# Gated linear attention: a head's output norm placed behind the next head's first score factors, one multiplication per step

## The chip, the cores and the metric

The kernel runs on one core of a Trainium2 chip. The metric is the device time of one execution in microseconds (us), taken as the median of several runs. Before the change it is 2079.0 us (three runs, 2078.53 to 2080.28).

The engines have these names in the profile: PE is TensorE's matmul, PEld its weight load, DVE is VectorE, ACT is ScalarE, POOL is GpSimd, SP is the queue that issues most DMAs.

## What is computed

One layer of a trunk: a gated linear attention mixer (512 tokens, model width 2048, 4 heads with 256 key and 512 value columns) and a SwiGLU feed-forward. The part that matters here is the mixer, cut to its core:

```python
def gla_mixer(h, w_in, w_a2, b_a, g_norm, w_out):
    q, k, v, r, a_lr = split(h @ w_in)
    log_a = log_sigmoid(a_lr @ w_a2 + b_a) / GLA_TAU
    ...
    scores = einsum('bhtd,bhsd,bhtsd->bhts', qb, kb, decay)   # decay = exp(b_t - b_s), s <= t
    o_intra = einsum('bhts,bhsv->bhtv', scores, vb)
    ...
    o = rms_norm(o, g_norm).reshape(B, S, GLA_DV) * silu(r)   # per head, over its 512 value columns
    return o @ w_out
```

The output norm of a head is `rms_norm(o)`: a sum of squares over the head's 512 value columns, the inverse root of their mean, and a multiplication of every output element with it.

## The kernel before

All of a head is done for the 512 tokens at once, with scores for every pair of tokens; no state is carried. Each head goes through these steps:

- `project_qk(h)`: 8 chunks of two weight tiles each, of 24 matmuls per chunk, into four banks; then VectorE writes q and k (L303, L305).
- `log_gate(h)` and `decays(h, b)`: the running sums of the log gates (tile PX, extended from level to level by `advance`: GpSimd L339, VectorE L340, by turns) and the exponentials made from them (kt for the keys, qt for the queries: L351 to L361).
- `scores(h, ...)`: in four levels, for blocks of 2, 8, 32 and 128 tokens. In each, `factors` multiplies the exponentials with k on GpSimd (kt, L406) and with q on VectorE (qt, L407 to L409); `products` are the matmuls of kt and qt on TensorE (L436, for the last level L495), and `take` copies them under a mask into the score tile Sd (VectorE, L454 and L458). The diagonal is a product by itself (GpSimd L417 and L418, TensorE L423, VectorE L425). "First factors" and "first products" below are those of blocks of 2, the second those of blocks of 8.
- `project_v(h)`: again 8 chunks, for the values.
- `attend(h, ...)`: scores times values into oT[h], with the sum of squares in the tile so. At its end it appends `finish`, the head's output norm: a matmul of so with ones (`rms_rows`, L215), then `rsqrt` (VectorE L161, ScalarE L162 and L163, VectorE L164 to L167) into the tile Rh, then four multiplications of oT[h] with Rh on GpSimd (L540).

Every weight chunk comes by DMA as a raw tile and is split into two parts: hi (ScalarE, L121) and lo (VectorE, L122). Three such pairs are in flight.

What sets the order: the projections' matmuls are written straight through by `group`, and after every second column of a chunk (12 matmuls) it calls `tick()`. A tick takes one step from the generator in front of the list `queue` and one step from the one in front of the list `side`. `scores` and `attend` stand in `queue`; `finish`, the diagonal's `take` and the next head's `log_gate` stand in `side`, one behind the other. So head h's scores and head h-1's norm are written between the matmuls of head h's projections. Each engine works through its own instructions in the order in which they were written.

Pools that matter: products, norm sums and diagonals take turns in three PSUM banks (`mis_ps`); the tiles kt, qt, PX, so and Rh exist once each.

Of the kernel before, what the change touches and what calls it, by code (L numbers as in the profile page):

```python
# [18 lines left out]
H = 4  # L19
# [22 lines left out]
def trunk_kernel(ctx: ExitStack, tc: tile.TileContext, x, xT, cst, masks, wa2r, w_in, w_out, w_gu, w_down, out):  # L42
# [22 lines left out]
    def mis_bank():  # L65
        return mis_ps.tile([P, G], F32, tag="mis", name="mis")

    def temp(n=S):
        return tmp.tile([P, S], F32, tag="t", name="t", bufs=4)[:, 0:n]
# [61 lines left out]
    def prod3(out, a, b, start, stop):  # L131
        (ah, al), (bh, bl) = a, b
        nc.tensor.matmul(out, ah, bh, start=start, stop=False)  # L133
        nc.tensor.matmul(out, ah, bl, start=False, stop=False)  # L134
        nc.tensor.matmul(out, al, bh, start=False, stop=stop)  # L135
# [22 lines left out]
    def rsqrt(src_ps, n, y, temps=None):  # L158

        a, t = temps or (temp(y.shape[1]), temp(y.shape[1]))  # L160
        nc.vector.tensor_scalar(a, src_ps, 1.0 / n, EPS, ALU.mult, ALU.add)  # L161
        nc.scalar.activation(t, a, AF.Ln)  # L162
        nc.scalar.activation(y, t, AF.Exp, scale=-0.5)  # L163
        nc.vector.tensor_mul(t, y, y)  # L164
        nc.vector.tensor_mul(t, t, a)
        nc.vector.tensor_scalar(t, t, -0.5, 1.5, ALU.mult, ALU.add)
        nc.vector.tensor_mul(y, y, t)  # L167
# [5 lines left out]
    def add_square(dst, src, first):  # L173
        if first:
            nc.gpsimd.tensor_mul(dst, src, src)
        else:
            sq = temp()
            nc.scalar.activation(sq, src, AF.Square)
            nc.gpsimd.tensor_add(dst, dst, sq)
# [33 lines left out]
    def rms_rows(src, n, dst):  # L213
        b = mis_bank()
        nc.tensor.matmul(b, ones, src, start=True, stop=True)  # L215
        yield
        rsqrt(b, n, dst)
# [72 lines left out]
        yield  # L290


    scored = []

    def project_qk(h):

# [98 lines left out]
    def scores(h, q, k, sc):  # L395
# [18 lines left out]
        def diagonal():  # L414
            e = temp()
            ev = e.rearrange("p (c t) -> p c t", c=2)
            nc.gpsimd.tensor_mul(ev, q[:, :, 0:S:2], k[:, :, 0:S:2])  # L417
            nc.gpsimd.tensor_add(e[:, 0:256], e[:, 0:256], e[:, 256:512])  # L418
            return e
# [43 lines left out]
        f = factors(2, *first_decays[h])  # L463
        yield
        e = diagonal()
        m0 = 0
        for b in LEVELS:
            advance(h, b)
# [42 lines left out]
    def attend(h, v, sc):  # L511
        (vh, vl, v3), (Sd, Sh, Sl) = v, sc
        ot = ob.tile([P, 4, G], F32, tag=f"ob{h}", name=f"oT{h}")
        oT.append(ot)
        so = gl.tile([P, S], F32, tag="so", name="so")

        def take(vt, b):
            nc.scalar.activation(oT[h][:, vt, :], b, AF.Copy)
            add_square(so, oT[h][:, vt, :], vt == 0)

        b = None
        for vt in range(4):
            prev, b = b, mis_bank()
            vs = slice(vt * P, (vt + 1) * P)
            for j, o in enumerate((0, 512, 896)):
                r = slice(o, o + (4 - j) * P)
                prod3(b[:, j * P :], (vh[:, j, vs], vl[:, j, vs]), (Sh[:, r], Sl[:, r]), j == 0, False)
            nc.tensor.matmul(b[:, 384:512], v3[:, vs], Sd[:, 384:512], start=False, stop=True)
            if prev is not None:
                take(vt - 1, prev)  # L530
            yield
            yield
        take(3, b)

        def finish():
            Rh = gl.tile([P, S], F32, tag="Rh", name="Rh")
            yield
            yield from rms_rows(so, HV, Rh)
            for vt in range(4):
                nc.gpsimd.tensor_mul(oT[h][:, vt, :], oT[h][:, vt, :], Rh)  # L540

        side.append(finish())

    queue.append(start())
    gates, oT, first_decays = [], [], []
    for h in range(H):
        q, k = project_qk(h)
        if h == 0:
            queue.append(log_gate(h))
        Sc = (  # L550
            gl.tile([P, S], F32, tag="Sd", name="Sd"),
            gl.tile([P, 1152], F32R, tag="Sh", name="Sh"),
            gl.tile([P, 1152], F32R, tag="Sl", name="Sl"),
        )
        queue.append(scores(h, q, k, Sc))
        v = project_v(h)
        queue.append(attend(h, v, Sc))
# [630 lines left out]
```

## Time and profile before

| | |
|---|---|
| median of three runs | 2079.0 us |
| the profiled execution, its own time | 2078.67 us |
| its span, first to last instruction | 2076.9 us |
| PE busy | 2063.1 us, 99% |
| DVE busy | 1597.9 us, 77% |
| ACT busy | 938.2 us, 45% |
| POOL busy | 313.5 us, 15% |
| mean granted TensorE clock | 0.998 |

A view by stretch gives, for each piece of the span, its length and each engine's busy time in it with the number of instructions in brackets, then the granted TensorE clock as a share of full speed, the DMA share and the rate. A row of the timeline is: start, duration, engine, line, operation, output tile and input tiles, shapes, count, and in square brackets how long the engine had been idle and what ended that. Rows of equal instructions in sequence are merged, their count behind the x. A list of waits gives the total, the number and the longest. All times are us from the start of the span. Head 0's scores lie at about 85 to 135 us, those of heads 1, 2 and 3 in the stretches 135 to 240, 240 to 345 and 345 to 450.

### The profile page before, as it was taken

How to read it: one execution, taken by the hardware profiler on the slowest of the kernel's cores; microseconds unless marked ns; L12 is line 12 of the kernel's file. 1: busy time of each engine (PE TensorE's matmuls, PEld its weight loads, DVE VectorE, ACT ScalarE, POOL GpSimd, SP SyncE). 2: the span in 40 equal slices, each digit the busy share in tenths (PEclk: the TensorE clock that was granted, in tenths of full speed). 3: DMA queues.
4: the chain of work that ended last, by engine and by line, in shares of the span. 5: the costliest groups of instructions: out<-in, count | busy, mean ns of one | idle time of the engine just before them, and what ended most of it. 6: DMA issues, size and time to landing. Idle time of an engine off the chain costs nothing.

```text
span 2076.9 us, 24516 instructions
## 1 busy us (share of the span) xinstructions
PE 2063.1 (99%) x9314; PEld 1712.3 (82%) x9314; DVE 1597.9 (77%) x1778; ACT 938.2 (45%) x1165; POOL 313.5 (15%) x315
## 2 busy tenths in 40 slices
PE   9998999999999999999999999999999999999999
PEld 8887888888887887888888888888888888888887
DVE  7765666655448899788788788788788787888887
ACT  6342424233325556545445445445445454333333
POOL 6324242423111220001001001001001010000000
PEclk9999999999999999999999999999999999999999
DMA  6221322224784885553553553553555676675632
GB/s 212 81 82 51 92 71 81 82 81 136 250 321 137 321 268 207 163 175 116 174 177 115 176 176 112 177 177 113 176 178 163 222 279 244 222 274 196 232 136 100
DMA packets 161333, 350.22 MB, mean 169 GB/s; under 512 B 14400, under 2 KB 30912, under 8 KB 161216
## 3 DMA queue, kind: packets, MB, share of 16 engines
q1 hardware_dynamic: 136704, 274.76, 39.8%
q0 software_dynamic: 21440, 71.84, 10.2%
q10 hardware_dynamic: 3072, 2.06, 0.3%
q8 instruction: 73, 1.20, 0.2%
q14 instruction: 44, 0.36, 0.0%
HBM read 279.93 MB, written 68.68 MB: 168 GB/s over the span
## 4 chain that ended last, share of the span: by engine, by line
PE 96%; DVE 2%; POOL 1%; ACT 0%; issue 0%; DMA 0%; SPq 0%; DVEq 0%; ACTq 0%
PE bank L1107 22%; PE bank L1108 22%; PE bank L1106 22%; PE acc L134 8%; PE acc L133 8%; PE acc L135 8%; PE mis L436 2%; PE bank L801 1%; DVE lo L707 1%; DVE raw L697 1%; PE mis L495 1%; PE mis L135 0%; PE mis L133 0%; PE mis L134 0%; DVE hs L824 0%; POOL oT L540 0%
## 5 line engine op out<-in xcount | busy, mean ns | idle before, releaser
L706 ACT CAST hi<-raw 128x1024 fp32r<-128x1024 f32 x518 | 544.7, 1054 | 684.3 <-PE bank L1108 578.6
L707 DVE TENSOR_TENSOR lo<-raw,hi 128x1024 fp32r<-128x1024 f32 x518 | 630.2, 1220 | 202.0 <-ACT hi L706 199.4
L1107 PE MATMUL bank<-lo,fe 128*128 128x512 f32 x1184 | 462.8, 391 | 2.7 <-DVE lo L707 2.6
L1106 PE MATMUL bank<-hi,fe 128*128 128x512 f32 x1184 | 463.8, 392 | 0.1
L1108 PE MATMUL bank<-hi,fe 128*128 128x512 f32 x1184 | 461.7, 390 | 0.0
L697 DVE TENSOR_TENSOR raw<-raw 128x1024 f32<-128x1024 f32 x296 | 359.9, 1216 | 2.4 <-DMA raw<-w_down 2.2
L1106 PE MATMUL bank<-hi,fl 128*128 128x512 f32 x888 | 345.8, 389 | 0.0
L1108 PE MATMUL bank<-hi,fl 128*128 128x512 f32 x888 | 345.6, 389 | 0.0
L1107 PE MATMUL bank<-lo,fl 128*128 128x512 f32 x888 | 345.6, 389 | 0.0
L1107 PEld LDWEIGHTS bank<-lo,fe 128*128 128x128 f32 x1184 | 222.7, 188 | 51.3 <-DVE lo L707 6.3
L1106 PEld LDWEIGHTS bank<-hi,fe 128*128 128x128 f32 x1184 | 222.8, 188 | 46.1 <-ACT hi L706 0.5
L1108 PEld LDWEIGHTS bank<-hi,fe 128*128 128x128 f32 x1184 | 222.6, 188 | 46.1
L122 DVE TENSOR_TENSOR lo<-raw,hi 128x1024 fp32r<-128x1024 f32 (+1 forms) x97 | 132.9, 1377 | 152.6 <-ACT hi L121 139.8
L133 PE MATMUL acc<-x,hi 128*128 128x512 f32 x512 | 203.4, 397 | 0.2 <-ACT x L170 0.2
L134 PE MATMUL acc<-x,hi 128*128 128x512 f32 x512 | 199.8, 390 | 0.3 <-DVE x L171 0.3
L121 ACT CAST hi<-raw 128x1024 fp32r<-128x1024 f32 (+1 forms) x97 | 100.9, 1040 | 218.5 <-PE acc L134 125.1
L135 PE MATMUL acc<-x,lo 128*128 128x512 f32 x512 | 199.6, 390 | 0.0
L1107 PEld LDWEIGHTS bank<-lo,fl 128*128 128x128 f32 x888 | 166.7, 188 | 35.7
L1106 PEld LDWEIGHTS bank<-hi,fl 128*128 128x128 f32 x888 | 166.7, 188 | 35.3 <-issue 0.6
L1108 PEld LDWEIGHTS bank<-hi,fl 128*128 128x128 f32 x888 | 166.7, 188 | 34.2
L838 POOL DMA_DIRECT2D hF<-hh x44 | 33.0, 749 | 787.6 <-ACT hs L828 691.5
L133 PEld LDWEIGHTS acc<-x,hi 128*128 128x128 f32 x512 | 96.3, 188 | 20.9 <-issue 1.0
(208 smaller groups left out, 2090.0 us busy)
## 6 DMA issues: line engine op xcount, KB each, us to landing
raw<-w_gu SPq DMA_DIRECT2D x176, 512.0 KB, 4.3
raw<-w_down SPq DMA_DIRECT2D x88, 512.0 KB, 5.3
raw<-w_in SPq DMA_DIRECT2D x64, 512.0 KB, 3.9
fe<-hF SPq DMA_DIRECT2D x44, 512.0 KB, 5.6
fl<-hF SPq DMA_DIRECT2D x33, 512.0 KB, 6.4
raw<-w_out SPq DMA_DIRECT2D x32, 512.0 KB, 8.3
raw<-w_in SPq DMA_DIRECT2D x62, 256.0 KB, 3.1
gF<-st POOLq DMA_DIRECT2D x48, 256.0 KB, 5.7
```

Of the source, the lines that this page charges most:

```text
L121: nc.scalar.copy(hi[:, c], raw[:, c])
L122: nc.vector.tensor_sub(lo[:, c], raw[:, c], f32(hi[:, c]))
L133: nc.tensor.matmul(out, ah, bh, start=start, stop=False)
L134: nc.tensor.matmul(out, ah, bl, start=False, stop=False)
L135: nc.tensor.matmul(out, al, bh, start=False, stop=stop)
L436: nc.tensor.matmul(bk[:, g * w : (g + 1) * w], kt[:, c, gg * P : (gg + 1) * P], qt[:, o : o + w], start=c == 0, stop=c == 1,)
L697: (nc.vector.tensor_add if ph == 5 else nc.vector.tensor_sub)(to, a, b)
L706: nc.scalar.copy(hi, raw)
L707: nc.vector.tensor_sub(lo, raw, f32(hi))
L1106: nc.tensor.matmul(o, ah, bh, start=a and begin, stop=False, skip_group_check=True)
L1107: nc.tensor.matmul(o, ah, bl, start=False, stop=False, skip_group_check=True)
L1108: nc.tensor.matmul(o, al, bh, start=False, stop=z, skip_group_check=True)
```

## The change

`scores` now notes in a list `factored` that a head's first factors and diagonal have been written. `finish` of head h, before its matmul and its root, gives its steps away until that has happened for head h+1 (for the last head the condition is met from the start). And the four multiplications are now four steps with a yield behind each, where they were written in one step. Everything that stands behind `finish` in the list `side` (the diagonal's `take` of the next head) moves back by as many steps.

```diff
-    scored = []
+    scored, factored = [], []
...
         f = factors(2, *first_decays[h])
         yield
         e = diagonal()
+        factored.append(h)
         m0 = 0
...
         def finish():
             Rh = gl.tile([P, S], F32, tag="Rh", name="Rh")
             yield
+            while len(factored) < min(h + 2, H):
+                yield
             yield from rms_rows(so, HV, Rh)
             for vt in range(4):
                 nc.gpsimd.tensor_mul(oT[h][:, vt, :], oT[h][:, vt, :], Rh)
+                yield
```

The instructions are the same; their order on the engines is not. The lines behind the edits are one to four numbers higher than before (L540 is now L543). GpSimd in head 1, from the end of head 0's sum of squares, before; oT_1105 is head 0's output:

```order
L179 TENSOR_TENSOR so<-so,t 128x512 x3
L540 TENSOR_TENSOR oT_1105<-oT_1105,Rh 128x512 x4
L402 MEMSET Sd 128x512
L406 TENSOR_TENSOR kt<-kt,k 128x1024
L411 COPY qt<-q 128x128x4
L417 TENSOR_TENSOR t<-q,k 128x512
L418 TENSOR_TENSOR t<-t 128x256
L339 TENSOR_TENSOR PX<-PX 128x256x2
L339 TENSOR_TENSOR PX<-PX 128x128x4
L406 TENSOR_TENSOR kt<-kt,k 128x1024
L339 TENSOR_TENSOR PX<-PX 128x64x8
```

GpSimd at the same place, now:

```order
L402 MEMSET Sd 128x512
L406 TENSOR_TENSOR kt<-kt,k 128x1024
L411 COPY qt<-q 128x128x4
L417 TENSOR_TENSOR t<-q,k 128x512
L418 TENSOR_TENSOR t<-t 128x256
L339 TENSOR_TENSOR PX<-PX 128x256x2
L339 TENSOR_TENSOR PX<-PX 128x128x4
L543 TENSOR_TENSOR oT_1105<-oT_1105,Rh 128x512 x2
L406 TENSOR_TENSOR kt<-kt,k 128x1024
L543 TENSOR_TENSOR oT_1105<-oT_1105,Rh 128x512
L339 TENSOR_TENSOR PX<-PX 128x64x8
```

The four multiplications have left their place ahead of the first kt and qt; two stand ahead of the second kt, one behind it, and the fourth two rows further down. VectorE in head 2, from the last step of PX before the second factors (L352 to L409), before:

```order
L340 TENSOR_TENSOR PX<-PX 128x128x4
L122 TENSOR_TENSOR lo<-raw,hi 128x1024 x2
L352 TENSOR_TENSOR qt<-PX 128x32x16
L357 TENSOR_TENSOR qt<-qt,PX 128x32x8
L407 TENSOR_TENSOR qt<-qt,q 128x32x24
L408 TENSOR_TENSOR qt<-qt,q 128x32x16
```

VectorE at the same place, now:

```order
L340 TENSOR_TENSOR PX<-PX 128x128x4
L122 TENSOR_TENSOR lo<-raw,hi 128x1024
L161 TENSOR_SCALAR t<-mis 128x512
L164 TENSOR_TENSOR t<-Rh 128x512
L165 TENSOR_TENSOR t<-t 128x512
L166 TENSOR_SCALAR t<-t 128x512
L167 TENSOR_TENSOR Rh<-Rh,t 128x512
L122 TENSOR_TENSOR lo<-raw,hi 128x1024
L352 TENSOR_TENSOR qt<-PX 128x32x16
```

The five VectorE instructions of the norm, which stood ahead of q and k in heads 2 and 3 and just behind k in head 1, now stand between the two lo tiles ahead of L352, in all three heads. On ScalarE, Ln and Exp (L162, L163) have moved likewise, to the place one hi tile ahead of the second exponentials.

## Prediction

> **What bounds the kernel now.** I read the page's busy shares first, then the busy time by stretch, then TensorE's waits, then the timelines of single engines around the one wait that this shows.
>
> ```profile
> span 2076.9 us, 24516 instructions
> PE 2063.1 (99%) x9314; PEld 1712.3 (82%) x9314; DVE 1597.9 (77%) x1778; ACT 938.2 (45%) x1165; POOL 313.5 (15%) x315
> ...
> 135.00:240.00 105.00, 99.72 (x464) 83.45 (x463) 64.12 (x87) 40.03 (x57) 38.09 (x24) 0.98 0.24 71
> 240.00:345.00 105.00, 105.00 (x496) 88.68 (x495) 64.80 (x84) 36.94 (x49) 37.10 (x24) 1.00 0.27 81
> 345.00:450.00 105.00, 105.00 (x493) 88.49 (x492) 66.45 (x86) 38.51 (x52) 36.23 (x23) 1.00 0.27 81
> ...
> PE mis L436 <- POOL qt L411: 5.3, 1, 5.3
> ```
>
> TensorE is busy 99% of the span, so a time is gained or lost only where TensorE waits. The three stretches (length, then busy time of PE, PEld, DVE, ACT, POOL, granted clock, DMA) are the scores of heads 1, 2 and 3. Heads 2 and 3 have no TensorE idle time at all. Head 1 has one wait, the last line (total, times, longest): the first products of scores wait for GpSimd.
>
> ```profile
> 174.22 7.27 POOL L540 TENSOR_TENSOR oT<-oT,Rh 128x512 f32<-128x512 f32 x4 [14.61 <-DVE Rh L167]
> 181.43 0.52 POOL L402 MEMSET Sd<- 128x512 f32 x1
> 181.92 2.33 POOL L406 TENSOR_TENSOR kt<-kt,k 128x1024 f32<-128x1024 f32 x1
> 184.20 0.62 POOL L411 COPY qt<-q 128x512 f32<-128x512 f32 x1
> ...
> 179.21 0.39 PE L135 MATMUL acc<-hi,x 128*128 128x512 f32 x1
> 184.87 5.32 PE L436 MATMUL mis<-qt,kt 128*128 128x256 f32 x16 [5.28 <-POOL qt L411]
> 294.47 3.61 PE L436 MATMUL mis<-qt,kt 128*128 128x256 f32 x16
> 309.30 2.76 PE L436 MATMUL mis<-qt,kt 128*128 128x192 f32 x16
> ```
>
> Rows are start, duration, engine, line. Four multiplications of head 0's output norm hold GpSimd for 7.27 us; head 1's own factors (kt, then qt) stand behind them and end at 184.82. The rows 294.47 and 309.30 are the first and second products of head 2, reached without a wait. The first products of head 1 take 5.32 us, those of head 2 only 3.61; why is in the clock:
>
> ```profile
> 181.30:184.75 3.45, 0.00 (x0) 0.00 (x0) 0.00 (x0) 0.00 (x0) 3.45 (x4) 1.00 0.00 0
> 184.75:188.15 3.40, 3.28 (x8) 2.66 (x9) 0.00 (x0) 0.00 (x0) 3.32 (x4) 0.50 0.00 0
> ...
> 642.11:645.53 3.42, 1.76 (x7) 0.92 (x6) 3.18 (x4) 2.92 (x5) 0.00 (x0) 1.00 0.00 0
> 645.53:648.94 3.41, 3.41 (x9) 2.65 (x10) 3.38 (x5) 2.45 (x5) 2.38 (x3) 0.50 0.29 47
> ```
>
> After the idle 3.45 us the granted clock (third last number) is 0.50 for 3.4 us. The same happened once more, after a stretch with TensorE busy for 1.76 of 3.42 us. So a long wait is paid twice.
>
> **What the stall is worth.** Back-to-back these matmuls start some 0.22 us apart (the stretch 240 to 345 holds no gap), so without the wait the first products of head 1 would start at 179.43, not at 184.87: 5.44 us. The half clock adds 5.32 - 3.61 = 1.71 us. The change takes the four multiplications from in front of kt and qt, so both go: **-7.15 us**. That nothing else is late at 179.43 follows from head 2, whose norm was out of the way in time:
>
> ```profile
> 168.75 0.69 DVE L305 TENSOR_TENSOR k<-acc,R 128x512 f32<-128x512 f32 x1 [0.68 <-PE acc L135]
> 283.79 0.69 DVE L305 TENSOR_TENSOR k<-acc,R 128x512 f32<-128x512 f32 x1 [0.67 <-PE acc L135]
> ```
>
> Head 2's key is ready at 284.48 and its first products start 9.99 us later unhindered; head 1's is ready at 169.44, and 179.43 is 9.99 us later. With the norm gone from in front, head 1 runs like head 2.
>
> **What takes its place.** The norm moves, in heads 1, 2 and 3 alike, to just behind the first factors. That is the stretch in which VectorE and GpSimd make the factors of the second products. VectorE's norm and what it is put in front of:
>
> ```profile
> 169.36 0.68 DVE L161 TENSOR_SCALAR t<-mis 128x512 f32<-128x512 f32 x1
> 171.53 0.69 DVE L164 TENSOR_TENSOR t<-Rh 128x512 f32<-128x512 f32 x1 [1.49 <-ACT Rh L163]
> ...
> 173.45 0.69 DVE L167 TENSOR_TENSOR Rh<-Rh,t 128x512 f32<-128x512 f32 x1
> ...
> 295.65 0.69 DVE L340 TENSOR_TENSOR PX<-PX 128x512 f32<-128x512 f32 x1 [1.38 <-POOL PX L339]
> 296.26 2.35 DVE L122 TENSOR_TENSOR lo<-raw,hi 128x1024 fp32r<-128x1024 f32 x2
> ...
> 300.01 2.73 DVE L407 TENSOR_TENSOR qt<-qt,q 128x768 f32<-128x768 f32 x1 [0.34 <-ACT qt L360]
> 302.66 1.65 DVE L408 TENSOR_TENSOR qt<-qt,q 128x512 f32<-128x512 f32 x1
> ...
> 305.70 0.45 DVE L458 COPY_PREDICATED Sd<-mk,mis 128x128 f32<-128x128 uint8 x1
> ...
> 299.32 2.60 POOL L406 TENSOR_TENSOR kt<-kt,k 128x1024 f32<-128x1024 f32 x1 [3.71 <-ACT kt L351]
> 301.88 1.87 POOL L339 TENSOR_TENSOR PX<-PX 128x512 f32<-128x512 f32 x1
> ```
>
> Head 2 before: after L340 VectorE makes two lo tiles (the second from about 297.4), then the factors (L352 to L409), then takes the first products out of their first bank, done with L458 at 306.15. The second products need those factors and that bank (three banks go round: norm, two products, diagonal, then the first product bank again). TensorE arrives at 309.30, so the slack is **3.15 us**, and the change puts two things in front of L458.
>
> First, the norm's five VectorE instructions, between the two lo tiles. From L161's start to L167's end they take 174.14 - 169.36 = 4.78 us, the 1.49 us of waiting for ScalarE's Ln and Exp included; VectorE works in order, so the second lo, L352 and all behind them wait through it. Its neighbours start 0.08 before the one ahead ends (296.26 against L340's end at 296.34), so it moves them by 4.70.
>
> Second, GpSimd's multiplications, which now run while VectorE makes the factors. The price of that meeting is in the rows:
>
> ```profile
> L540 POOL TENSOR_TENSOR oT<-oT,Rh x16: 1282/1296/2267, 174.2 to 493.0; 128x512 f32<-128x512 f32 x16
> ...
> 175.19 2.06 DVE L407 TENSOR_TENSOR qt<-qt,q 128x768 f32<-128x768 f32 x1
> 177.16 1.78 DVE L408 TENSOR_TENSOR qt<-qt,q 128x512 f32<-128x512 f32 x1
> 178.86 1.50 DVE L409 TENSOR_TENSOR qt<-qt,q 128x256 f32<-128x256 f32 x1
> ...
> 197.75 0.95 DVE L407 TENSOR_TENSOR qt<-qt,q 128x768 f32<-128x768 f32 x1
> 198.75 0.69 DVE L408 TENSOR_TENSOR qt<-qt,q 128x512 f32<-128x512 f32 x1
> 199.36 0.42 DVE L409 TENSOR_TENSOR qt<-qt,q 128x256 f32<-128x256 f32 x1
> ...
> 299.25 0.42 DVE L357 TENSOR_TENSOR qt<-qt,PX 128x256 f32<-128x256 f32 x1
> ...
> 313.46 2.52 DVE L357 TENSOR_TENSOR qt<-qt,PX 128x256 f32<-128x256 f32 x1
> 313.30 2.39 POOL L406 TENSOR_TENSOR kt<-kt,k 128x1024 f32<-128x1024 f32 x1 [4.03 <-ACT kt L351]
> ```
>
> A multiplication lasts 1282 ns at least (minimum, median and maximum of 16). Beside the first four (174.22 to 181.49) L407, L408 and L409 take 2.06, 1.78 and 1.50 us; with GpSimd quiet 0.95, 0.69 and 0.42. Each time it is 1.1 us more: the engines take turns, one instruction each. Behind a kt, L357 takes 2.52 for 0.42, 2.1 us more; behind L339, L408 takes 1.65 for 0.69, 1.0 more.
>
> Now the sum for head 2. Before, 306.15 holds 1.78 of L407 behind kt (2.73 - 0.95), 0.96 of L408 behind L339 and 0.34 of waiting for ScalarE; without them 303.07. With the norm 307.77. Rh is then ready at 297.4 + 4.78, near 302.2, just as the second lo runs, and GpSimd has five instructions to do: two oT, kt, one oT, L339. VectorE has five as well: L352, L357, L407, L408, L409. Taking turns they cost VectorE 3 x 1.1 + 2.1 + 1.0 = 6.4 us: 307.77 + 6.4 = **314.2**. TensorE stands at the second products from 309.30 to 314.2: **a new wait of 4.9 us**. However that falls on the 3.41 us stretches of the clock's rows, one of them holds at least half of it, 2.45 us, and so has TensorE busy for less than 1.0 us, well under the 1.76 that was enough; a half clock follows, for another 1.71. The heads differ by nothing in this: heads 2 and 3 have equal busy rows, and head 1 follows head 2's distances.
>
> Own time of the profiled execution 2078.67 (span 2076.9 and 1.8 around it): 2078.67 - 7.15 + 3 x (4.9 + 1.71) = 2091.35. The median of the three runs lies 0.33 above that execution, so **2091.7 us**.
>
> **Costed at nothing.** TensorE's norm sum and the diagonal's matmul move back some 24 to 96 matmuls and keep their length. Ln and Exp on ScalarE are inside the 4.78; one hi tile and the exponentials for the second kt now stand behind them, beside VectorE's last four steps of the norm (171.53 to 174.14, 2.6 us) and the second lo, so that Rh and not they should hold GpSimd; if they don't fit, kt comes later still, which the upper end holds. The second lo tile, at 303.3 instead of 298.6, is used only behind the second products. The fourth multiplication falls into the third products' factors; the delay of the second products moves their due time by the same 4.9 us, and if that cover fails it costs one more turn, 1.1 us a head, which I keep for the upper end. No DMA changes its place in a queue; the weight load that waits for that lo's raw buffer is issued as much later as the lo ends, two tiles ahead of its use. Head 3's own norm has no condition to wait for, and no row of it moves.
>
> **Two rules of the Trainium skill.** On the turns: "SBUF — State Buffer", section "Who interferes with whom", says that VectorE with two SBUF inputs and a GpSimd instruction that reads SBUF hold one shared port for a whole instruction each, the other fully blocked. The trace agrees in kind; its 1.1 and 2.1 us are somewhat under the whole instructions (1.28 undisturbed, kt 2.39), since part of each runs before the turn is over. With whole ones a head's turns would cost 3 x 0.18 + 0.29 = 0.8 us more, and the sum would be 2094.2. On the clock: "TensorE: Matmul & The Clock Gate", section "What's actually happening", has the clock halved after an idle window of about 3.4 us. The rows at 642.11 show it halved after a window that was half busy. What it would make of the time is rival (c).
>
> **Rivals.** (a) *The stall goes and nothing comes.* The factors of the second products keep up, since heads 2 and 3 have 3.15 us of slack. Then only -7.15 counts: 2071.9. It needs the norm and the turns together to cost VectorE less than 3.15 us, against 4.70 for the norm alone; only VectorE time that is free already, in waits I don't see, could make that. This is the other side: faster. (b) *The norm counts, the turns don't grow.* The second products are ready at 307.77 + 1.78 + 0.96 = 310.5, a wait of 1.2 us, too short to halve the clock: -7.15 + 3 x 1.2 gives 2075.4, within 0.2%. For it: the turns before cost 2.7 us too; against it: the three oT are in the queue right there. The balance tips where a head's new wait and half clock pass 7.15 / 3 = 2.4 us. (c) *The clock is halved only after a whole idle stretch.* The old wait held one, from 181.30 to 184.75. A wait of 4.9 us would hold one in (4.9 - 3.41) / 3.41 = 44% of placements: -7.15 + 3 x (4.9 + 0.44 x 1.71) gives 2088.8. Against it stands the row at 642.11. (d) *The change does not do what it says* is out: the order's rows show both moves.
>
> **How the numbers follow.** Forecast 0.66, (c) 0.16, (a) 0.09, (b) 0.09. Forecast's own ends: one turn fewer and half of a half clock, 3 x (3.8 + 0.85), is 2085.8; one turn more and two half clocks in part, 3 x (6.0 + 2.2), is 2096.4. The range is drawn to 2082 to 2096.5, so that it takes in waits down to some 3.4 us a head in all. About 0.2% (4.2 us) is what a measurement here can tell from no change; by that, (a) is faster, (b) the same, the forecast and (c) slower: 0.09, 0.09, 0.82.
>
> **What would show it.** Right: no TensorE wait at head 1's first products; one wait of some 5 us at the second products (the ones with 192 columns) of each of heads 1 to 3, put down to VectorE; L407 to L409 there at 1.5 to 3 us beside L543; a granted clock of 0.50 after each. Wrong: TensorE's busy time equal to the stretch in all three, L409 of the second factors done by 308; or the old wait still in place.

## The result, and the profile after

The changed kernel takes 2090.89 us (median of four runs, 2088.29 to 2090.98), the kernel before 2078.82 us (2078.53 to 2080.28): a ratio of 1.0052, 95% interval 1.0040 to 1.0065. It is slower, by half a per cent. The profiled execution of the changed kernel has an own time of 2090.88 us.

The page's first lines, the busy time in the stretches of heads 1 to 3 and TensorE's waits in them, of the changed kernel:

```profile
span 2089.1 us, 24513 instructions
PE 2068.3 (99%) x9314; PEld 1717.2 (82%) x9314; DVE 1611.0 (77%) x1778; ACT 937.7 (45%) x1165; POOL 317.5 (15%) x315
...
135.00:240.00 105.00, 101.31 (x474) 85.77 (x473) 69.91 (x87) 40.61 (x58) 38.47 (x24) 0.98 0.25 71
240.00:350.00 110.00, 106.31 (x494) 89.76 (x494) 68.57 (x84) 36.11 (x48) 39.30 (x24) 0.98 0.26 77
350.00:460.00 110.00, 106.30 (x485) 89.75 (x484) 70.23 (x85) 38.63 (x52) 37.93 (x23) 0.97 0.25 72
...
PE mis L436 <- DVE Sd L458: 11.1, 3, 3.7
```

The old wait for GpSimd is gone. In its place TensorE waits three times for 3.7 us, once per head, now for VectorE's L458: the instruction that clears the first product bank. Heads 2 and 3, where TensorE was busy without a break before, have lost 3.7 us of it each. VectorE's busy time has grown by 13 us with the same 1778 instructions; single instructions have become longer, as the rows further down show.

TensorE's timeline at the products of heads 1, 2 and 3 (start, duration, engine, line), and the clock in the stretches behind the waits of heads 2 and 3:

```profile
181.49 2.75 PE L436 MATMUL mis<-qt,kt 128*128 128x256 f32 x12
...
200.17 4.52 PE L436 MATMUL mis<-qt,kt 128*128 128x192 f32 x16 [3.69 <-DVE Sd L458]
...
309.38 0.39 PE L135 MATMUL acc<-hi,x 128*128 128x512 f32 x1
313.45 4.30 PE L436 MATMUL mis<-qt,kt 128*128 128x192 f32 x16 [3.69 <-DVE Sd L458]
...
422.42 0.39 PE L135 MATMUL acc<-hi,x 128*128 128x512 f32 x1
426.50 5.46 PE L436 MATMUL mis<-qt,kt 128*128 128x192 f32 x16 [3.70 <-DVE Sd L458]
...
313.05:316.46 3.41, 3.01 (x10) 3.04 (x11) 2.10 (x7) 0.00 (x0) 1.15 (x2) 0.50 0.00 0
...
425.66:429.08 3.42, 2.58 (x8) 2.61 (x9) 2.48 (x7) 0.00 (x0) 0.72 (x1) 0.50 0.00 0
429.08:432.49 3.41, 3.41 (x12) 3.31 (x11) 3.00 (x3) 0.43 (x1) 1.60 (x2) 0.50 0.00 0
```

Head 1's first products (181.49) run without a wait; its second products (200.17) have the new one. Head 2's second products could have started at 309.38 + 0.23 and start at 313.45, 3.84 us late; then they take 4.30 us at half clock where 2.76 were enough before. In head 3 the half clock lasts for two stretches of 3.41 us, and the products take 5.46.

VectorE and GpSimd in head 2, from the norm to L458:

```profile
296.80 0.68 DVE L161 TENSOR_SCALAR t<-mis 128x512 f32<-128x512 f32 x1
300.81 0.69 DVE L167 TENSOR_TENSOR Rh<-Rh,t 128x512 f32<-128x512 f32 x1
301.42 1.22 DVE L122 TENSOR_TENSOR lo<-raw,hi 128x1024 fp32r<-128x1024 f32 x1
302.56 1.78 DVE L352 TENSOR_TENSOR qt<-PX 128x512 f32<-128x512 f32 x1
304.37 1.40 DVE L357 TENSOR_TENSOR qt<-qt,PX 128x256 f32<-128x256 f32 x1
305.70 3.15 DVE L407 TENSOR_TENSOR qt<-qt,q 128x768 f32<-128x768 f32 x1
308.77 1.77 DVE L408 TENSOR_TENSOR qt<-qt,q 128x512 f32<-128x512 f32 x1
310.47 1.36 DVE L409 TENSOR_TENSOR qt<-qt,q 128x256 f32<-128x256 f32 x1
312.87 0.44 DVE L458 COPY_PREDICATED Sd<-mk,mis 128x128 f32<-128x128 uint8 x1
...
301.58 3.91 POOL L543 TENSOR_TENSOR oT<-oT,Rh 128x512 f32<-128x512 f32 x2 [6.56 <-DVE Rh L167]
305.45 2.58 POOL L406 TENSOR_TENSOR kt<-kt,k 128x1024 f32<-128x1024 f32 x1
308.00 1.99 POOL L543 TENSOR_TENSOR oT<-oT,Rh 128x512 f32<-128x512 f32 x1
309.96 1.59 POOL L339 TENSOR_TENSOR PX<-PX 128x512 f32<-128x512 f32 x1
```

The norm holds VectorE from 296.80 to 301.50, 4.70 us. Then each of VectorE's five factor instructions (L352 to L409) gives way to one of GpSimd's five: their durations add up to 9.46 us.

### The profile page after: what moved, and what is told of

Same layout as the page of the kernel before. It is cut to its first block, busy times and chain, and to the rows that moved or that the text cites. A ratio compares the mean times of both kernels' runs of the same rounds, so it can differ in the third digit from the quotient of the medians.

```text
span 2089.1 us, 24513 instructions
## 1 busy us (share of the span) xinstructions
PE 2068.3 (99%) x9314; PEld 1717.2 (82%) x9314; DVE 1611.0 (77%) x1778; ACT 937.7 (45%) x1165; POOL 317.5 (15%) x315
## 4 chain that ended last, share of the span: by engine, by line
PE 92%; DVE 5%; POOL 1%; issue 1%; ACT 1%; DMA 0%; SPq 0%; POOLq 0%; ACTq 0%; DVEq 0%
PE bank L1111 22%; PE bank L1112 22%; PE bank L1110 22%; PE acc L134 7%; PE acc L133 7%; PE acc L135 7%; PE mis L436 1%; PE bank L805 1%; DVE lo L711 1%; DVE raw L701 1%; PE mis L496 1%; DVE qt L407 0%; POOL PX L339 0%; PE mis L133 0%; PE mis L135 0%
## 5 line engine op out<-in xcount | busy, mean ns | idle before, releaser
L134 PE MATMUL acc<-x,hi 128*128 128x512 f32 x512 | 200.3, 391 | 0.3 <-DVE x L171 0.3
L135 PE MATMUL acc<-x,lo 128*128 128x512 f32 x512 | 200.4, 391 | 0.1
```

## The experiments

Theory: the norm's VectorE time (4.7 us) and the turns with three multiplications (3 x 1.1 = 3.3 us) add up in front of the second products, against a slack of 3.15 us. Rival A: the norm's VectorE instructions alone make the wait. Rival B: the turns alone make it. Each diff is against the changed kernel; each ratio is against the kernel before, run on the same chip, with its 95% interval.

**Multiplications away, root as changed** (mults_late).

```diff
+            multiply = mults(h, Rh)
+            if h < H - 1:
+                pending.append(multiply)
+            else:
+                yield from multiply
...
-            for vt in range(4):
-                nc.gpsimd.tensor_mul(oT[h][:, vt, :], oT[h][:, vt, :], Rh)
-                yield
...
             side.append(log_gate(h + 1))
+        side.extend(pending)
+        pending.clear()
```

> The norm's root stays where the change puts it; the four multiplications go behind the next head's scores, beside its attend, so that none of them meets the second factors. Theory (norm and turns add up, 4.7 and 3.3 us, against the slack): the wait at each head's second products falls from 3.7 to about 0.5 us, no half clock, and the time is 2078.8 - 7.15 + 3 x 0.5 = 2073.2. Rival A (the norm's VectorE instructions alone make the wait): it stays at 3.7 us with its half clock, near 2088. Rival B (the multiplications' turns alone make it): no wait, 2071.7.

Measured: 2077.40 us, ratio 0.9991 (0.9982 to 1.0000). TensorE's waits, and VectorE's lo tile and second factors in head 2:

```profile
PE mis L436 <- DVE Sd L458: 2.2, 3, 0.7
PE acc L133 <- DVE vl L324: 0.9, 1, 0.9
PE mis L134 <- DVE Sl L512: 0.8, 1, 0.8
```

```profile
294.96 3.42 DVE L122 TENSOR_TENSOR lo<-raw,hi 128x1024 fp32r<-128x1024 f32 x1
298.31 1.64 DVE L352 TENSOR_TENSOR qt<-PX 128x512 f32<-128x512 f32 x1
299.98 0.42 DVE L357 TENSOR_TENSOR qt<-qt,PX 128x256 f32<-128x256 f32 x1
300.32 0.95 DVE L407 TENSOR_TENSOR qt<-qt,q 128x768 f32<-128x768 f32 x1
301.32 0.69 DVE L408 TENSOR_TENSOR qt<-qt,q 128x512 f32<-128x512 f32 x1
301.93 0.42 DVE L409 TENSOR_TENSOR qt<-qt,q 128x256 f32<-128x256 f32 x1
```

With the multiplications gone the same five instructions take 4.12 us in place of 9.46. Not all of these 5.3 us are won: kt now meets the lo tile ahead of them, which takes 3.42 us in place of 1.22. That leaves 3.1 us, close to the 3.3 that three multiplications were put at, and the wait falls by 3.0, from 3.7 to 0.7: rival A is out. The time is 4 us above what was expected. Compared matmul by matmul with the profiled execution before, TensorE loses 3.1 us at the three second products, where 1.5 were expected, and 2.6 us in head 3 between 445 and 449 us, where the second and third wait lie. In head 3 no next log gate stands ahead of the multiplications, so on GpSimd three of them follow the last kt directly, earlier than was meant, and take turns with VectorE's last factors:

```profile
430.47 2.51 POOL L406 TENSOR_TENSOR kt<-kt,k 128x1024 f32<-128x1024 f32 x1 [1.60 <-ACT kt L351]
432.94 5.42 POOL L552 TENSOR_TENSOR oT<-oT,Rh 128x512 f32<-128x512 f32 x3
...
433.99 1.77 DVE L352 TENSOR_TENSOR qt<-PX 128x512 f32<-128x512 f32 x1
435.79 1.40 DVE L357 TENSOR_TENSOR qt<-qt,PX 128x256 f32<-128x256 f32 x1
437.12 2.05 DVE L407 TENSOR_TENSOR qt<-qt,q 128x768 f32<-128x768 f32 x1
```

**Root at its old place, multiplications as changed** (root_early).

```diff
+            yield from rms_rows(so, HV, Rh)
             while len(factored) < min(h + 2, H):
                 yield
-            yield from rms_rows(so, HV, Rh)
```

> The norm's matmul and root go back to their old place; only the four multiplications wait for the next head's first factors. Theory: without the norm's 4.7 us in front, the turns of four multiplications alone exceed the slack of 3.15 us by about 1.5 us in each head; head 1's first products wait about 1 us for VectorE, which has the norm in front of the first factors there: 2078.8 - 7.15 + 1.0 + 3 x 1.5 = 2077.2. Rival A (norm alone): no wait at the second products, 2072.7. Rival B (turns alone): the wait stays at 3.7 us with half clocks, 2088.

Measured: 2077.61 us, ratio 0.9993 (0.9983 to 1.0002).

```profile
PE mis L436 <- DVE Sd L458: 3.7, 3, 1.6
PE mis L436 <- DVE qt L409: 1.1, 1, 1.1
```

Three waits of 3.7 us in all (about 1.5 each were expected), and one of 1.1 at head 1's first products, as the theory has it. Rival B, which keeps 3.7 us per head, is out. The norm alone left a head a wait of 0.7 us, the multiplications alone one of 1.2 on average and 1.6 at most, neither with a half clock; together they leave 3.7 and a half clock.

**The condition alone** (one_step): the last `yield` behind the multiplication is taken out, so that all four stand ahead of the second kt.

> The condition alone: four multiplications in one step, all ahead of the second kt. Theory (turns, one instruction each): five GpSimd instructions still meet VectorE's five ahead of its last factor, four multiplications and kt instead of three, kt and one L339, 6.5 instead of 6.4 us: the wait stays at 3.7 to 3.9 us, the time at the change's 2090.9 (within 1.5). Rival (kt's own lateness decides: a multiplication more in front of kt makes the products later by a whole 1.2 us or more): 4.9 us a head, 2094.5.

Measured: 2089.98 us, ratio 1.0053 (1.0037 to 1.0070).

```profile
PE mis L436 <- DVE Sd L458: 11.4, 3, 3.8
```

The wait stays, though a fourth multiplication stands ahead of kt: it is the number of turns that counts, not which of GpSimd's instructions takes them. The yields make no difference to the changed kernel that these runs could tell.

**The yields alone** (yields_only): the two lines of the condition are taken out.

> The other part alone: no condition, the four multiplications one per step at the norm's old place. Heads 2 and 3 are then as before the change. Theory: in head 1 one multiplication stands ahead of kt instead of four, so the first products wait about 1.7 us, without a half clock; but the others then come between the first factors and the second kt, and the second products wait some 4 us: 2078.8 - 7.15 + 1.7 + 4 + 1.5 = 2078.9, no change that can be measured. Rival (only the four multiplications in a row cost anything): the wait is gone, 2073.

Measured: 2079.15 us, ratio 0.9996 (0.9987 to 1.0005), as expected.

```profile
PE mis L436 <- DVE Sd L458: 3.3, 1, 3.3
PE mis L436 <- DVE qt L409: 1.4, 1, 1.4
PE acc L134 <- DVE lo L122: 1.0, 1, 1.0
```

The one wait of 5.3 us is now three in head 1, 5.7 us in all: spread multiplications delay what stands behind each of them. The wait of 1.0 us, for a lo tile, was not foreseen.

**The change for the first norm alone** (first_head_only).

```diff
-            while len(factored) < min(h + 2, H):
+            while h == 0 and len(factored) < 2:
```

> The change for head 0's norm alone (in head 1's stretch); heads 2 and 3 keep the norm at its old place. Theory: -7.15 for the old wait, one new wait of 3.85 us with its half clock of 1.5: 2077.0; TensorE has no wait in heads 2 and 3. Rival (the cost is not the sum of three equal ones, but sits in one head): near 2072 or near 2083.

Measured: 2077.60 us, ratio 0.9990 (0.9981 to 1.0000).

```profile
PE mis L436 <- DVE Sd L458: 3.7, 1, 3.7
```

One wait instead of three, and a time near the expected 2077.0: the changed kernel's wait is three equal ones, one per head. What the half clock adds to each is not equal, as the table below shows.

**The sum matmul at its old place** (sum_early). It was to show why the wait is 3.7 us and not 4.9.

```diff
+            b = mis_bank()
+            nc.tensor.matmul(b, ones, so, start=True, stop=True)
+            yield
             while len(factored) < min(h + 2, H):
                 yield
-            yield from rms_rows(so, HV, Rh)
+            rsqrt(b, HV, Rh)
```

> As the change, but the norm's sum matmul is written at its old place, ahead of the condition; VectorE, ScalarE and GpSimd have the change's order. It tests why the new wait is 3.7 us where 4.9 were forecast. Theory: the sum matmul, moved to between the key and the second products, lets TensorE arrive 0.9 us later and so covers 0.9 us of VectorE's delay; put back, the wait is 4.6 us a head, and the time 2.7 us above the change's, 2093.6. Rival (its place does not matter, VectorE is simply ready earlier than worked out): 3.7 us and the change's time, 2090.9.

Measured: 2096.49 us, ratio 1.0081 (1.0066 to 1.0096), waits of 5.7 us. That is more than either expected, because the statement on the other engines' order was wrong: without the step that the matmul used up behind the condition, the root came a step earlier, ahead of both lo tiles, and three multiplications stood ahead of kt. It doesn't tell the two apart.

**The same with one more step given away** (sum_early_same_steps): a `yield` behind the condition.

> The sum matmul at its old place again, now with one step given away behind the condition, so that VectorE, ScalarE and GpSimd have exactly the change's order (in the run sum_early they had not: the root came a step sooner, ahead of both lo tiles, and three multiplications ahead of kt). Theory (the moved sum matmul covers 0.9 us of VectorE's delay): the wait at the second products is 3.7 + 0.9 = 4.6 us in each of heads 1 to 3, and the time some 2.7 us above the change's, 2093.6, with up to 1.5 more or less by half clocks. Rival (its place does not matter): 3.7 us and 2090.9.

Measured: 2092.37 us, ratio 1.0065 (1.0048 to 1.0082).

```profile
PE mis L436 <- DVE Sd L458: 13.7, 3, 4.6
```

4.6 us each, as expected: the moved sum matmul had covered 0.9 us. The time is 1.2 us below the expected 2093.6, inside the 1.5 allowed for half clocks. In the changed kernel's trace its price can be read off:

```profile
288.20 0.39 PE L135 MATMUL acc<-hi,x 128*128 128x512 f32 x1
288.43 1.02 PE L215 MATMUL mis<-so,ones 128*128 128x512 f32 x2
...
289.53 0.40 PE L134 MATMUL acc<-lo,x 128*128 128x512 f32 x1
```

From this L135 to the next L134, with one projection matmul and the sum between them, are 1.33 us, where two steps of 0.23 would do without the sum: it takes 0.9 us of TensorE, about four times a matmul of the projections.

**Root at its old place, multiplications away** (root_early_mults_late): the condition is taken out of mults_late.

> Norm's root at the old place, multiplications behind the next head's scores. Theory: no wait at the second products in any head; head 1's first products wait about 1 us for VectorE: 2072.7. Rival B (turns alone) also says no wait there; rival A as well; it tells what is left of the old wait when only the multiplications are taken out of its way.

Measured: 2073.02 us, ratio 0.9969 (0.9957 to 0.9981). One TensorE wait is left in heads 1 to 3, 1.1 us at head 1's first products, for VectorE's L409, which has the norm in front of it there.

**The whole norm beside the next head's attend** (norm_late): `finish` without the condition is handed over by the list `pending` of mults_late, behind the next head's scores, and so exists twice.

```diff
-        side.append(finish())
+        if h < H - 1:
+            pending.append(finish())
+        else:
+            side.append(finish())
...
-        so = gl.tile([P, S], F32, tag="so", name="so")
+        so = gl.tile([P, S], F32, tag="so", name="so", bufs=2)
```

> The whole norm (matmul, root and multiplications) is written behind the next head's scores, beside its attend, where GpSimd and VectorE have free time; the tile of the sum of squares exists twice for that. Theory: neither the old nor the new wait is there, TensorE is busy through all of heads 1 to 3: 2078.8 - 7.15 = 2071.7. Rival (taking the norm out of one place only moves the wait, since attend needs the same engines): a wait of 2 to 4 us in each head's attend, 2078 or more.

Measured: 2071.47 us (five runs), ratio 0.9961 (0.9948 to 0.9973), faster than the kernel before and the changed one.

```profile
135.00:240.00 105.00, 105.00 (x500) 89.14 (x500) 65.08 (x87) 44.20 (x61) 33.73 (x22) 1.00 0.26 76
240.00:345.00 105.00, 105.00 (x496) 88.62 (x496) 65.24 (x85) 37.06 (x51) 36.17 (x24) 1.00 0.27 81
345.00:450.00 105.00, 105.00 (x492) 88.20 (x491) 65.05 (x85) 36.17 (x48) 33.59 (x22) 1.00 0.26 76
```

TensorE is busy through all three stretches, at full clock: the norm fits where no product is waiting for VectorE and GpSimd. It gains 7.7 us on the kernel before as run on the same chip (2071.47 against 2079.18); the old wait with its half clock was put at 7.15.

## Why the prediction was right

| term | forecast | the two profiled executions |
|---|---|---|
| old wait gone | -5.44 | -5.44 |
| its half clock gone | -1.71 | -1.71 |
| new waits | 3 x 4.9 = 14.7 | 3 x 3.84 = 11.5 |
| their half clocks | 3 x 1.71 = 5.1 | 1.5 + 1.5 + 3.0 = 6.0 |
| sum in heads 1 to 3 | 12.7 | 10.4 |
| elsewhere | 0 | 1.8 |
| all | 12.7 | 12.2 |

- **The stall's worth.** Right: norm_late has neither the old wait nor a new one in heads 1 to 3, and gains 7.7 us for 7.15.
- **A new wait at the second products of each head, for VectorE.** Right in place, number and cause. Both parts of the sum were shown to be needed: 0.7 us with the norm alone, 1.2 on average (3.7 / 3) with the multiplications alone.
- **The norm's 4.70 us and the turns' 6.4.** From L161's start to the start of the lo behind L167 the norm took 4.62 (296.80 to 301.42). The turns took 9.46 less the 3.16 that L352 to L409 need undisturbed (0.68, 0.42, 0.95, 0.69 and 0.42), 6.3.
- **The size of the wait.** Mis-sized: 4.9 forecast, 3.84 measured. The term that failed is in the part costed at nothing: "TensorE's norm sum and the diagonal's matmul move back some 24 to 96 matmuls and keep their length." They do, but the sum now stands between the key and the second products, so TensorE itself comes 0.9 us later and waits that much less (4.6 with the sum put back). The rest, some 0.2, fits ScalarE's trip, 1.42 us for 1.49, and the turns, 6.3 for 6.4; no run takes these apart.
- **One half clock of 1.71 per wait.** The forecast took the row at 642.11 against rival (c), and the clock was halved behind all three waits. Head 3 speaks against rival (c): the half clock begins at 425.66, and the stretch of 3.41 us ahead of it, from 422.25, was not wholly idle, since a matmul of 0.39 us starts in it at 422.42. In head 3 the clock was halved for two stretches and cost twice as much, which the forecast had only in its upper end.
- **The balance.** The median is 0.8 us below the forecast, closer than its terms allow, and that is luck: waits 3.2 too long, half clocks 0.9 too short, and 1.8 us elsewhere that the change does not explain. Of these 2.0 lie in the first 66 us, where the order of the two kernels is the same (below).

## What to carry to other kernels

Work that is taken from in front of one wait has to be put where both of its engines have slack, and the slack is that of the next deadline, not of the engine's average: here two parts that each almost fitted into the slack of 3.15 us (waits of 0.7 and 1.2 us alone) cost three waits of 3.7 together. In these traces VectorE's and GpSimd's element-wise instructions, where both had some to do, took turns one by one, at about 1.1 us for each multiplication and 2.1 for each kt, so work on an engine with free time is not free for its neighbour. And a step in the program is no time on the chip: what is written behind something else runs as early as its own engine reaches it, as head 3 in mults_late shows.

## What the runs showed of the hardware beyond that

Whether a short wait is followed by a half clock differs from one execution to the next. Both kernels have the same wait of 1.5 us, ending at 645.4 us before and at 657.95 now. Before, it fell into a stretch with 1.76 us of TensorE work, and a half clock followed. In the changed kernel's execution the stretches fell like this:

```profile
654.35:657.77 3.42, 1.91 (x8) 1.01 (x6) 2.84 (x3) 2.92 (x4) 0.00 (x0) 1.00 0.00 0
657.77:661.18 3.41, 3.01 (x12) 2.17 (x12) 3.38 (x5) 2.45 (x5) 2.39 (x3) 1.00 0.22 33
...
5.80:9.20 3.40, 2.31 (x9) 1.10 (x8) 2.83 (x5) 2.63 (x6) 0.00 (x0) 1.00 0.82 299
9.20:12.60 3.40, 3.40 (x9) 2.62 (x10) 2.54 (x3) 1.55 (x3) 0.00 (x0) 0.50 0.73 209
```

With 1.91 us of work in the stretch the clock stays up. The busy time of a stretch alone does not settle it, though: at the start of the same execution a stretch with 2.31 us is followed by a half clock. And head 3's stretch at 425.66, at half clock with 2.58 us of work, is followed by another, while after head 2's at 313.05, with 3.01, the clock is back. What exactly the clock goes by stays open.

The half clock at the start, which the profiled execution before has not, made all that follows 2.0 us later (the first log gate matmul starts at 67.9 for 65.9). One of the four runs came out 2.6 us below the others at a mean clock of 0.998 for their 0.996 and 0.997, which would fit fewer half clocks; it left no trace to show it. Waits of 0.7 to 1.6 us at the products (mults_late, root_early) were followed by no half clock, those of 3.3 us and more (yields_only, the changed kernel and the runs with longer waits) by one or two stretches each. So some 2 us of a difference between two executions of this kernel can be the clock alone; the waits in the trace are the firmer evidence.
